# A tuned transformer-layer kernel: own staging tiles for the weights, recurrence steps apart from their norm and gate, another order of the heads' columns

## The chip, the cores and the metric

The kernel runs on one core of a Trainium2 chip. The metric is the device time of one execution in microseconds (us), as the median of several runs. Five engines work side by side and meet only at semaphores: TensorE (PE), VectorE (DVE), ScalarE (ACT), GpSimd (POOL) and SyncE (SP), which issues nearly all DMAs here.

## The reference, cut to what matters

One layer (D = 1024) over 2048 latent rows after a 256-row context. The change touches the first of its three parts, the mixers:

```python
h = modulate(rmsnorm(x, norm_mix), sh1, sc1)
p = h @ w_in                                   # 3584 columns
# A: 4 heads of a gated recurrence, one scan per direction, 128x128 state per head
logf_f, k_f, logf_b, k_b, v = hgrn2_gates(p, ...)
q = silu(p[..., 3*w:4*w]) * HG_DIM ** -0.5
o = rmsnorm(o_f + flip_t(o_b)); o_hg = o * silu(p[..., 4*w:5*w])
# B: 4 heads of a gating unit over chunks of 128 rows
o_mlp = chunk_sgu(p[..., 5*w:6*w], p[..., 6*w:], ...)   # gelu(u) * (W_s LN(gelu(v)) + b)
x = x + g1 * (concat(o_hg, o_mlp) @ w_out)
h2 = modulate(rmsnorm(x, norm_ffn), sh2, sc2)
x = x + g2 * conv_ffn(h2, w_up, conv_w, conv_b, w_down)
```

`g1`, `g2`, `sh1` and so on come from `silu(c) @ w_ada + b_ada`.

## The kernel before, in words

Rows are taken in two halves of 1024 (`hh` 0 and 1). A matmul in full precision is made of three products of split numbers (`mm3`, L128): high part by high part, high by low, low by high. One **pass** of `run_banks` (L503) is one block of 128 columns of `w_in` by 512 rows: 8 slices of k by three products, 24 matmuls of 128x512, into one of three PSUM tiles `pj`. Two passes make a column block of a half. For a head h of group A the blocks are g (the output gate, into `sgt`), t (the values, into `vt`), q (into `qs`) and the two forget gates, four passes in turn, called b here (into `F` and `K`); of group B they are v and u. Before the change the string for a half says `f` for g, t, q in this order (L1071, L1092).

**Weights.** `split_w` (L210) turns 128 columns of `w_in` from a raw tile of 512 KB into `whi` (ScalarE cast, L125) and `wlo` (VectorE difference, L126). There are two such pairs, so a block is split when the pair before the last is free. All raw tiles (`raw_tile`, L200) come from one ring of three, which `w_in` shares with the background work. The load (L207) is traced with the split, unless context columns are near.

**Side work.** Between slices of k, `slot()` (L177) gives two pumps a turn. Each pump holds generators; a generator does a step, then yields a wait in us of PE work (`T.t`, a planned clock of PE alone), after which its next step is due. `hg_q` runs the recurrence of a head (`hg`, L741): score products for seven levels of blocks, each with DVE and ACT updates of Q and K, then transposes, chunk states, a chain over the chunks on DVE (L733, L739), and the outputs. In the first half the outputs of the forward scan, the states of the backward scan, Q and the gate go to DRAM; in the second half `deferred(h)` (L849), a generator of its own behind `hg`, finishes head h of the first half. `o_norm` (L704) squares on ACT, asks POOL for 1/sqrt (L118, L120) and scales on DVE (L713); `o_gate` (L717), 6.5 us later by the pump, transposes and gates. `later(fn, wait)` runs a piece once it is due: the transposes of the values (L576 to L582, due after 2.2), the LayerNorm of group B (`ln`, due after 4.6) and its mixing product (`mix`, 7.0 after that). `bg_q` holds the background: x, then eight blocks of `w_ada`, the taps, `w_down` times g2 (L956, to `wd_d`), `w_out` times g1 and its split (L940, L125, L126, to `wo_d` at L942 and L943).

**Forced steps.** `need(q, what)` runs steps of a pump at once, without their waits, until `what` is done: the keys of the head before at the start of each b (`pre_g`), the scores of the diagonal blocks at q, the end of the head two before at g. `open_wo` (L1103) drains both pumps four passes before the end and then loads the rest of `w_out`; three tiles of it (`wo_early`, L847) are loaded within the last head.

**Order.** The program is traced in this order, and a planner then orders the instructions of each engine by its own estimate of when each is ready; an instruction in `pin(...)` stays behind the one traced before it on its engine. Each engine runs its queue in order, SP too: a store that waits for its data holds back every load behind it. After the first half's last pass, xh and xl, the split rows, are loaded anew from DRAM, 16 loads of 512 KB (L1058, L1059).

Of the kernel before, what the change touches and what calls it, by code (L numbers as in the profile page):

```python
# [18 lines left out]
P = 128  # L19
# [58 lines left out]
def tile_trunk(ctx, tc, x, c, cx, c_ctx, w_ada, b_ada, norm_mix, norm_ffn, w_in, hg_norm, sgu_g, sgu_b,  # L78
# [104 lines left out]
    with es1:  # L183
# [16 lines left out]
        def raw_tile():  # L200
            return p1.tile([P, D], F32, tag="raw", name="raw", bufs=3)
# [3 lines left out]
        def load_raw(key):  # L205
            raw = raw_tile().rearrange("p (k c) -> p k c", c=P)
            ld(raw, w_in[:, key[0]:key[0] + P].rearrange("(k p) c -> p k c", p=P))  # L207
            w_raw[key] = raw

        def split_w(key, eng=None):  # L210
            if key not in w_raw:
                load_raw(key)
            raw, at = w_raw.pop(key), w_free.pop(0)
            hi = p1.tile([P, NK, P], F32R, tag=f"whi{at}", name="whi", align_bytes=AL)
            lo = p1.tile([P, NK, P], F32R, tag=f"wlo{at}", name="wlo", align_bytes=AL)
            split(hi, lo, raw, eng or V)
            return hi, lo, at

# [109 lines left out]
        with tc.manual_schedule():  # L328
# [44 lines left out]
            nxt[0, CTX] = split_w((0, CTX), V)  # L373
# [4 lines left out]
            nxt[HW, CTX] = split_w((HW, CTX), V)  # L378
# [125 lines left out]
        def run_banks(banks, peek=None):  # L504
# [3 lines left out]
            for i, (col, n0, n, sink, pre) in enumerate(banks):  # L508
                if pre is not None:
                    pre()  # L510
                up = list(dict.fromkeys(keys[i:] + tail))
                for key in up[:2]:
                    if key not in nxt:
                        nxt[key] = split_w(key)
# [7 lines left out]
                for k in range(k0, NK):  # L522
                    if k and n == 512:
                        slot()
                    w_products(pj[:, :n], (hi, lo), hiT, loT, sl, k, k + 1)
# [129 lines left out]
        def sgu(hh, h):  # L655
# [14 lines left out]
            def sv(n0, n, pj):  # L670
# [3 lines left out]
                def ln():  # L674
# [10 lines left out]
                    nm = pm.tile([P, 4], F32, tag="nm", name="nm", bufs=2)  # L685
                    V.scalar_tensor_tensor(out=nm, in0=mv[:, :, 0], scalar=-1.0, in1=r[:, :4], op0=ALU.mult, op1=ALU.mult)
                    for i in range(4):
                        S.activation(nt[:, i * P:(i + 1) * P], pt[:, i * P:(i + 1) * P], AF.Identity,
                                     bias=nm[:, i:i + 1], scale=r[:, i:i + 1])

                    def mix():
# [8 lines left out]
                        both(n0)  # L700
                    hg_q.later(mix, 7.0)
# [3 lines left out]
        def o_norm(o):  # L705

            ss = ph.tile([P, 4], F32, tag="oss", name="oss", bufs=2)
            for i in range(4):
# [3 lines left out]
            on = ph.tile([P, 512], F32, tag="on", name="on", bufs=2)  # L712
            V.tensor_mul(on.rearrange("p (c q) -> p c q", q=P), o.rearrange("p (c q) -> p c q", q=P),  # L713
                         view(r, 0, [[1, 4], [0, P]]))
            return on

        def o_gate(hh, h, g0, on, sg):  # L717

            pt = bank("mi")
            for i in range(4):  # L720
                T.transpose(pt[:, i * P:(i + 1) * P], on[:, i * P:(i + 1) * P], ident)
            ot = pm.tile([P, 512], F32, tag="ot", name="ot", bufs=2)
            V.scalar_tensor_tensor(out=ot, in0=pt, scalar=hgn[:, h:h + 1], in1=sg[:, g0:g0 + 512],
                                   op0=ALU.mult, op1=ALU.mult)
            st(oT_d[hh][:, h, g0:g0 + 512], ot)
# [16 lines left out]
        def hg(hh, h, F, K, qs, vt, sgt):  # L742
# [6 lines left out]
            sc = ph.tile([P, NCH, P], F32, tag="S", name="sc")  # L749
# [17 lines left out]
            tot = F  # L767
            for l, B in enumerate(LV):
                if B < SB:
# [28 lines left out]
            yield 2.5  # L798
            fs = ph.tile([P, NCH + 1, P], F32, tag="fs", name="fs")
# [20 lines left out]
            on = []  # L820
            for g in range(0, NCH, 4):
# [9 lines left out]
                if hh == 1:  # L831
                    on.append(o_norm(po))
# [935 lines left out]
```

## Time and profile before

| | us |
|---|---|
| median of 3 runs | 2435.43 (2433.93 to 2435.67) |
| the profiled execution | 2435.89 |
| its span, first to last instruction | 2434.1 |
| projections and mixers (w_in) | about 32 to 952 |
| product with w_out | from about 952 |

The page's shares are averages over three parts with different limits; the change touches the first. PE counts as busy for the modelled length of its matmuls, which overlap, so a PE at 97% has little idle time but says nothing of how dense the rest is. What is lost is read from the waits of PE and from the granted clock, which is 1.00 at 2.4 GHz and 0.50 at 1.2 GHz.

### The profile page before, as it was taken

To read this page: it belongs to the slowest core of one execution; us is meant where nothing else is said; L and a number is where in the kernel's file an instruction comes from. 1 tells how busy PE (TensorE), PEld (TensorE's weight loads), DVE (VectorE), ACT (ScalarE), POOL (GpSimd) and SP (SyncE) were. 2 spreads that over 40 slices of the span, in tenths; PEclk is the share of its full clock that TensorE was granted. 3 is DMA by queue.
4 is the path that set the end of the run, shared out by engine and by line. 5 is a ranking of instruction groups with operands and counts; after the bars stand their busy time and mean duration, and the time that the engine had idled before them with its cause. 6 is when DMAs were issued, how large, how long until landed. Compare 5 with 4: busy or idle time off the path is not lost.

```text
span 2434.1 us, 38863 instructions
## 1 busy us (share of the span) xinstructions
PE 2362.0 (97%) x14951; PEld 1938.0 (80%) x14951; DVE 1703.7 (70%) x2323; ACT 1027.8 (42%) x1776; POOL 791.2 (33%) x739
## 2 busy tenths in 40 slices
PE   6999999999999898999999999999999999999998
PEld 4887887878887777888788888878888878888887
DVE  4656675465577573566898787679999983676876
ACT  4665544444454552454433333333333333332253
POOL 0010000000000121002687878778787860000011
PEclk9999999999999999999999999999999999999999
DMA  8454453563436536678622222552222248843744
GB/s 303 131 191 157 133 166 126 186 216 132 140 130 201 179 109 243 195 217 281 222 93 91 83 89 84 200 212 87 95 84 90 89 162 320 294 135 130 251 153 172
DMA packets 306295, 400.08 MB, mean 164 GB/s; under 512 B 33705, under 2 KB 216753, under 8 KB 302397
## 3 DMA queue, kind: packets, MB, share of 16 engines
q1 hardware_dynamic: 302820, 396.84, 48.8%
q8 instruction: 118, 1.93, 0.3%
q10 hardware_dynamic: 3289, 0.76, 0.1%
q14 instruction: 68, 0.56, 0.1%
HBM read 288.40 MB, written 109.13 MB: 163 GB/s over the span
## 4 chain that ended last, share of the span: by engine, by line
PE 40%; DVE 7%; POOL 2%; issue 2%; DMA 1%; ACT 1%; SPq 0%; POOLq 0%; ACTq 0%; DVEq 0%
PE up L70 23%; PE dn L70 17%; DVE dn L1348 3%; DVE edges L1353 1%; POOL Al L126 1%; DMA raw<-in_w_up_dram 1%; DVE gp L1424 1%; ACT dn L1345 1%; DMA yfar<-yd 0%; POOL raw L1174 0%; DVE keep L1434 0%; DVE keep L1418 0%; ACT cv L1367 0%; POOL fl L1170 0%; ACT Ah L125 0%
## 5 line engine op out<-in xcount | busy, mean ns | idle before, releaser
L1348 DVE SCALAR_TENSOR_TENSOR dn<-gp,taps,dn 128x1024 f32<-128x1024 f32 x352 | 448.1, 1279 | 21.0 <-ACT dn L1345 17.8
L70 PE MATMUL up<-yfar,Ah 128*128 128x512 f32 x1232 | 394.3, 390 | 2.8 <-DMA yfar<-yd 2.8
L70 PE MATMUL dn<-thl,mhl 128*128 128x512 f32 x1680 | 381.0, 389 | 0.0
L70 PE MATMUL pj<-xh,whi 128*128 128x512 f32 x896 | 368.1, 411 | 8.3 <-ACT whi L125 8.2
L126 POOL TENSOR_TENSOR Al<-raw,Ah 128x512 fp32r<-128x512 f32 x264 | 343.7, 1310 | 89.5 <-ACT Ah L125 84.1
L70 PEld LDWEIGHTS dn<-thl,mhl 128*128 128x128 f32 x1680 | 315.3, 188 | 65.5 <-issue 0.2
L70 PE MATMUL pj<-xl,whi 128*128 128x512 f32 x896 | 353.8, 395 | 0.0
L70 PE MATMUL pj<-xh,wlo 128*128 128x512 f32 x896 | 353.6, 395 | 0.2 <-DVE wlo L126 0.2
L70 PE MATMUL up<-xah,Al 128*128 128x512 f32 x704 | 275.9, 392 | 3.7 <-POOL Al L126 3.7
L125 ACT CAST Ah<-raw 128x512 fp32r<-128x512 f32 x264 | 160.4, 618 | 277.4 <-PE up L70 212.7
L70 PE MATMUL up<-xah,Ah 128*128 128x512 f32 x704 | 275.2, 391 | 2.0 <-ACT Ah L125 2.0
L70 PEld LDWEIGHTS up<-yfar,Ah 128*128 128x128 f32 x1232 | 231.4, 188 | 51.3 <-DMA yfar<-yd 3.2
L70 PEld LDWEIGHTS pj<-xh,whi 128*128 128x128 f32 x896 | 170.0, 190 | 45.3 <-ACT whi L125 9.1
L70 PE MATMUL up<-xal,Ah 128*128 128x512 f32 x528 | 205.7, 390 | 0.0
L70 PE MATMUL up<-yfar,Al 128*128 128x512 f32 x528 | 205.2, 389 | 0.0
L70 PEld LDWEIGHTS pj<-xh,wlo 128*128 128x128 f32 x896 | 169.8, 190 | 37.6 <-DVE wlo L126 0.9
L70 PEld LDWEIGHTS pj<-xl,whi 128*128 128x128 f32 x896 | 170.6, 190 | 30.6 <-DVE xl L126 0.2
L70 PE MATMUL dn<-wo,o 128*128 128x512 f32 x768 | 184.7, 397 | 3.7 <-DMA wo<-wo_d 2.8
L70 PEld LDWEIGHTS dn<-wo,o 128*128 128x128 f32 x768 | 143.0, 189 | 34.0 <-DMA wo<-wo_d 3.7
L126 DVE TENSOR_TENSOR wlo<-raw,whi 128x1024 fp32r<-128x1024 f32 x68 | 83.1, 1222 | 121.9 <-ACT whi L125 120.6
L70 PEld LDWEIGHTS up<-xah,Al 128*128 128x128 f32 x704 | 132.6, 188 | 35.5 <-POOL Al L126 8.2
L70 PEld LDWEIGHTS up<-xah,Ah 128*128 128x128 f32 x704 | 132.6, 188 | 30.4 <-ACT Ah L125 3.1
(322 smaller groups left out, 3664.6 us busy)
## 6 DMA issues: line engine op xcount, KB each, us to landing
raw<-in_w_up_dram SPq DMA_DIRECT2D x88, 512.0 KB
mr<-m SPq DMA_DIRECT2D x85, 512.0 KB
raw<-in_w_in_dram SPq DMA_DIRECT2D x68, 512.0 KB
sT<-wd SPq DMA_DIRECT2D x88, 256.0 KB
raw<-in_w_ada_dram SPq DMA_DIRECT2D x32, 512.0 KB
yfar<-yd SPq DMA_DIRECT2D x14, 1024.0 KB
m<-cv SPq DMA_DIRECT2D x22, 544.0 KB
raw<-in_w_down_dram SPq DMA_DIRECT2D x22, 512.0 KB
```

The costliest lines, as they stand in the source:

```text
L70: return self.engine.matmul(out, lhsT, rhs, **kw)
L125: keep(S.copy(hi, raw))
L126: (eng or G).tensor_sub(lo, raw, hi.bitcast(F32))
L1345: S.activation(cr, gt[:, 0:RH, 0:GW], AF.Identity, bias=cvb[:, f:f + 1], scale=taps[:, f:f + 1])
L1348: V.scalar_tensor_tensor(out=cr, in0=gt[:, t // 3:t // 3 + RH, t % 3:t % 3 + GW], scalar=taps[:, t * NF + f:t * NF + f + 1], in1=cr, op0=A ...
L1353: V.scalar_tensor_tensor(out=e[:, 0, :], in0=gt[:, 1, t % 3:t % 3 + GW], scalar=taps[:, t * NF + f:t * NF + f + 1], in1=e[:, 0, :], op0=AL ...
L1424: V.tensor_add(g_rows(hh, f + c, n2), quad(p, kind), quad(add, kind))
```

## The change

- **Raw tiles.** `w_in` uses raw tile 0 alone once the background starts, the background tiles 1 and 2. The raw tile of the block after next is loaded in slice 6 of a pass, if no other raw weight is held.
- **Low part late.** `split_w` casts at the start of a pass; the difference on DVE is traced at slice 3, pinned (`late`), for a block that isn't the pass's own.
- **Norm and gate apart.** `o_out` takes the place of `o_norm` and `o_gate`: squares and 1/sqrt with the step, scaling 3.2 later, transposes and gate 2.6 after that, the store 2.0 after that. In group B, the rows of the LayerNorm that need POOL's result (`rows`) run 3.4 after `ln`. They are pinned.
- **Stores.** Most stores of this part go through `put`: traced pinned some us after their data.
- **First half's finishing in line.** `deferred` becomes the end of `hg(1, h)`, its gate in the `fs` tile; "end" is said behind it, "gated" when its gates are written.
- **Background.** Loads run two ahead and are pinned; each step is cut into smaller ones; g1 is loaded twice in place of 16 times (256 KB each); `w_out` goes by its column half first. `wo_load` now needs all of `w_out`'s preparation (`need(bg_q, "wo")`).
- **need** and `open_wo` also run every piece that `later` holds.
- **Order of columns.** First half: u3 is moved behind b3. Second half: q, t, b and g of a head in that order (for heads 1 to 3 t, q, b, g), and u0 ahead of b3.

The work computed is the same. The diff, cut to its core:

```diff
-        def raw_tile():
-            return p1.tile([P, D], F32, tag="raw", name="raw", bufs=3)
+        raws, turn = {"w": [0, 1, 2], "b": [1, 2]}, {"w": 0, "b": 0}
+
+        def raw_tile(use="b"):
+            turn[use] += 1
+            return p1.tile([P, D], F32, tag=f"raw{raws[use][(turn[use] - 1) % len(raws[use])]}", name="raw")
...
-            raw = raw_tile().rearrange("p (k c) -> p k c", c=P)
+            raw = raw_tile("w").rearrange("p (k c) -> p k c", c=P)
...
-        def split_w(key, eng=None):
+        w_late = []
...
+        def split_w(key, late=False):
...
-            raw, at = w_raw.pop(key), w_free.pop(0)
+            raw, at = w_raw[key], w_free.pop(0)
...
-            split(hi, lo, raw, eng or V)
+            S.copy(hi, raw)
+
+            def low():
+                i = V.tensor_sub(lo, raw, hi.bitcast(F32))
+                if late:
+                    pin(i)
+                del w_raw[key]
+            w_late.append(low)
+            if not late:
...
+        def split_low():
+            while w_late:
+                w_late.pop(0)()
+
+        def put(dst, src, wait=2.5):
+            hg_q.later(lambda: pin(st(dst, src)), wait)
...
                 up = list(dict.fromkeys(keys[i:] + tail))
+                split_low()
                 for key in up[:2]:
                     if key not in nxt:
-                        nxt[key] = split_w(key)
+                        nxt[key] = split_w(key, n == 512 and key != up[0])
...
+                        if k == 3:
+                            split_low()
+                        if k == 6 and len(up) > 2 and up[2] not in nxt and not w_raw:
+                            load_raw(up[2])
...
             while what not in done:
+                if hg_q.soon:
+                    hg_q.flush()
+                    continue
...
-                    st(oT_d[hh][:, 4 + h, n0:n0 + 512], zt)
+                    put(oT_d[hh][:, 4 + h, n0:n0 + 512], zt, 4.0)
...
-                    nm = pm.tile([P, 4], F32, tag="nm", name="nm", bufs=2)
-                    V.scalar_tensor_tensor(out=nm, in0=mv[:, :, 0], scalar=-1.0, in1=r[:, :4], op0=ALU.mult, op1=ALU.mult)
...
-                        S.activation(nt[:, i * P:(i + 1) * P], pt[:, i * P:(i + 1) * P], AF.Identity,
...
+                    def rows():
+                        nm = pm.tile([P, 4], F32, tag="nm", name="nm", bufs=2)
+                        pin(V.scalar_tensor_tensor(out=nm, in0=mv[:, :, 0], scalar=-1.0, in1=r[:, :4], op0=ALU.mult,
+                                                   op1=ALU.mult))
+                        for i in range(4):
+                            pin(S.activation(nt[:, i * P:(i + 1) * P], pt[:, i * P:(i + 1) * P], AF.Identity,
...
+                    hg_q.later(rows, 3.4)
                     hg_q.later(mix, 7.0)
                 hg_q.later(ln, 4.6)
...
-        def o_norm(o):
+        def o_out(hh, h, g0, o, sg, what):
...
-            on = ph.tile([P, 512], F32, tag="on", name="on", bufs=2)
-            V.tensor_mul(on.rearrange("p (c q) -> p c q", q=P), o.rearrange("p (c q) -> p c q", q=P),
...
-            return on
...
+            def scaled():
+                on = ph.tile([P, 512], F32, tag="on", name="on", bufs=2)
+                pin(V.tensor_mul(on.rearrange("p (c q) -> p c q", q=P), o.rearrange("p (c q) -> p c q", q=P),
+                                 view(r, 0, [[1, 4], [0, P]])))
+
+                def gated():
+                    pt = bank("mi")
...
+                    put(oT_d[hh][:, h, g0:g0 + 512], ot, 2.0)
+                    if g0:
+                        done.add(what)
+                hg_q.later(gated, 2.6)
+            hg_q.later(scaled, 3.2)
...
+            sc = None
             for l, B in enumerate(LV):
+                if B == SB:
+                    sc = ph.tile([P, NCH, P], F32, tag="S", name="sc")
...
+            if hh and h and (0, h - 1, "gated") not in done:
+                hg_q.flush()
...
-                st(dh_d[h], bs_[:, :NCH, :].rearrange("p c t -> p (c t)"))
-                st(qb_d[h], Q[:, 0, :])
-                st(sg_d[h], sgt)
+                put(dh_d[h], bs_[:, :NCH, :].rearrange("p c t -> p (c t)"), 1.4)
+                put(qb_d[h], Q[:, 0, :], 1.4)
+                put(sg_d[h], its["sgt"], 1.4)
...
-                    on.append(o_norm(po))
+                    o_out(hh, h, g * P, po, lambda: its["sgt"], (hh, h, "gated"))
...
+                    put(op_d[h][:, g * P:g * P + 512], ot, 2.0)
                 yield 1.0
-            if hh == 1:
-                yield 6.5
-                for g in range(2):
...
+            if hh == 0:
+                return
+            Qb = ph.tile([P, 2, TH], F32, tag="Q", name="Qb", align_bytes=AL)[:, 0, :]
             op = ph.tile([P, TH], F32, tag="S", name="op")
-            bs_ = ph.tile([P, NCH + 1, P], F32, tag="bst", name="bs2")
-            ld(bs_[:, :NCH, :], dh_d[h].rearrange("p (c t) -> p c t", t=P))
-            ld(Qb, qb_d[h])
-            ld(op, op_d[h])
-            ld(sgt, sg_d[h])
...
+            sg = ph.tile([P, NCH + 1, P], F32, tag="fs", name="sg0")[:, :NCH, :].rearrange("p c t -> p (c t)")
...
+            for i, (j, cl) in enumerate(todo):
+                if j == 0:
+                    g = pm.tile([P, 512], F32, tag="acc", name="g2")
+                    pin(ld(g, g_d[1:2, cl].broadcast_to([P, 512])))
+                    yield 4.0
+                raw = raw_.pop(0)
+                pin(V.tensor_mul(raw, raw, view(g, 0, [[0, 2], [1, 512]])))
+                yield 4.0
+                pin(st(wd_d[j][:, :, cl], raw))
+                yield 4.0
+                load(i + 2)
+                yield 2.0
...
+            todo = [(k, slice(n * 512, n * 512 + 512)) for n in range(2) for k in range(NK)]
...
-                    raw = raw_tile()
-                    ld(raw[:, :512], w_out[k * P:(k + 1) * P, cl])
-                    ld(raw[:, 512:], g_d[0:1, cl].broadcast_to([P, 512]))
-                    raws.append(raw)
+                    raw_.append(raw_tile())
+                    pin(ld(raw_[-1][:, :512], w_out[k * P:(k + 1) * P, cl]))
...
+            load(1)
...
+                if k == 0:
+                    g = pm.tile([P, 512], F32, tag="acc", name="g1")
+                    pin(ld(g, g_d[0:1, cl].broadcast_to([P, 512])))
+                    yield 4.0
+                raw = raw_.pop(0)
+                w, hi = raw[:, :512], raw[:, 512:]
                 pin(V.tensor_mul(w, w, g))
-                split(hi.bitcast(F32R), g.bitcast(F32R), w, V)
-                st(wo_d[:, k, 0, cl], hi)
-                st(wo_d[:, k, 1, cl], g)
-                yield 7.0
-
...
+                pin(S.copy(hi.bitcast(F32R), w))
+                yield 1.6
+                pin(V.tensor_sub(w.bitcast(F32R), w, hi))
+                yield 2.2
+                pin(st(wo_d[:, k, 0, cl], hi))
+                pin(st(wo_d[:, k, 1, cl], w))
+                yield 3.0
+                load(i + 2)
...
+            def pre_s():
+                if before[0] >= 0:
+                    need(hg_q, (*before, "gated" if before[0] else "end"))
...
+                    raws["w"] = [0]
+                    bg_q.add(ada_blocks())
                     bg_q.add(conv_taps())
                     bg_q.add(w_down_ops())
-                    bg_q.add(w_out_ops())
+                    bg_q.add(marked(w_out_ops(), "wo"))
...
-                hg_q.add(marked(hg(hh, h, t["F"], t["K"], t["qs"], t["vt"], t["sgt"]), (hh, h, "end")))
-                if hh == 1:
-                    hg_q.add(deferred(h))
...
-        for item in "f1 v2 b1 f2 u2 b2 f3 v3 u3 b3".split():
...
-        run_banks(seq, 4 * HW)
+        rest, post = sequence(0, "b0 g1 t1 q1 v2 b1 g2 t2 q2 u2 b2 g3 t3 q3 v3 b3 u3", ctx_last)
...
+        run_banks(seq, 3 * HW)
...
-        for item in "f0 b0 f1 b1 f2 v0 b2 f3 b3 u0 v1 u1 v2 u2 v3 u3".split():
...
+        seq, post = sequence(1, "q0 t0 b0 g0 t1 q1 b1 g1 t2 q2 v0 b2 g2 t3 q3 u0 b3 g3 v1 u1 v2 u2 v3 u3", post)
...
-            hg_q.drain()
+            while hg_q.tasks:
+                hg_q.flush()
+                hg_q.step()
+            hg_q.flush()
             bg_q.drain()
+            hg_q.flush()
```

## Rows read from the trace of the kernel before

**Rows 1.** The page, part 1: busy us, share of the span and instructions of each engine.

```profile
PE 2362.0 (97%) x14951; PEld 1938.0 (80%) x14951; DVE 1703.7 (70%) x2323; ACT 1027.8 (42%) x1776; POOL 791.2 (33%) x739
```

**Rows 2.** The view of windows, all engines: busy us (xcount), clock, DMA share, GB/s.

```profile
1300.00:1400.00 100.00, 100.00 (x443) 82.84 (x442) 77.08 (x85) 36.45 (x58) 82.58 (x70) 1.00 0.26 85
503.00:511.00 8.00, 6.18 (x19) 4.30 (x18) 5.25 (x6) 3.71 (x4) 0.00 (x0) 0.79 0.62 212
757.00:767.00 10.00, 7.09 (x31) 5.58 (x30) 7.29 (x10) 2.98 (x6) 1.21 (x2) 0.83 0.61 201
822.00:836.00 14.00, 7.38 (x29) 5.94 (x28) 8.27 (x11) 4.19 (x5) 0.00 (x0) 0.76 0.93 276
951.00:965.00 14.00, 10.27 (x40) 7.75 (x40) 1.98 (x2) 1.21 (x3) 1.29 (x1) 0.88 1.04 382
```

**Rows 3.** The view of waits, PE, 480 to 965 us: us, times, longest.

```profile
PE pj L70 <- ACT whi L125: 8.2, 2, 6.6
PE mi L74 <- DVE on L713: 3.7, 4, 1.3
PE mi L74 <- ACT vv L576: 2.9, 1, 2.9
PE dn L70 <- DMA wo<-wo_d: 2.8, 2, 2.3
PE mi L70 <- ACT nt L688: 2.2, 2, 1.5
PE sc L70 <- DVE tot L500: 1.1, 1, 1.1
```

**Rows 4.** The view of waits, the SP queue, 250 to 960 us.

```profile
SPq L942 <- ACT wo_hi L125: 44.6, 13, 15.5
```

**Rows 5.** The view of waits, DVE, 250 to 960 us.

```profile
DVE wlo L126 <- ACT whi L125: 91.3, 22, 15.4
DVE on L713 <- POOL rs L120: 40.4, 16, 7.6
...
DVE nm L686 <- POOL rs L120: 16.1, 12, 2.6
```

**Rows 6.** The timeline, SP, 808 to 828 us: start, us, engine, line.

```profile
822.53 0.39 SPq L207 DMA_DIRECT2D raw<-in_w_in_dram  x1
```

**Rows 7.** The timeline, ACT, 757 to 763 us, then 815 to 834 us.

```profile
761.18 0.62 ACT L125 CAST wo_hi<-raw 128x512 fp32r<-128x512 f32 x1 [2.58 <-DVE raw L940]
761.71 0.58 ACT L576 COPY vv<-pj 128x512 f32<-128x512 f32 x1
...
829.03 1.04 ACT L125 CAST whi<-raw 128x1024 fp32r<-128x1024 f32 x1 [4.35 <-DMA raw<-in_w_in_dram]
```

**Rows 8.** The timeline, DVE, 526 to 552 us, then PE, 533 to 552 us.

```profile
534.63 1.23 DVE L126 TENSOR_TENSOR wlo<-raw,whi 128x1024 fp32r<-128x1024 f32 x1 [2.92 <-ACT whi L125]
...
542.64 1.22 DVE L493 TENSOR_TENSOR Q<-Q,tot 128x1024 f32<-128x1024 f32 x1
...
533.67 0.76 PE L70 MATMUL sc<-Q,K 128*32 128x32 f32 x64
...
548.07 0.40 PE L70 MATMUL pj<-xh,whi 128*128 128x512 f32 x1
```

**Rows 9.** The view of tile `wo_d` on SP: first and last start.

```profile
L943 SPq DMA_DIRECT2D wo_d<-raw x16: 319/320/520, 732.3 to 871.7; - x16
L847 SPq DMA_DIRECT2D wo<-wo_d x8: 319/386/648, 879.5 to 945.3; - x8
```

**Rows 10.** The view of tile `xh` on SP, and the timeline, PE, 503 to 508 us.

```profile
L1058 SPq DMA_DIRECT2D xh<-xh_d x8: 360/365/662, 475.9 to 490.9; - x8
...
505.65 0.50 PE L70 MATMUL pj<-xh,whi 128*128 128x512 f32 x1 [1.62 <-ACT whi L125]
```

**Rows 11.** The view of windows, 480 to 500 us.

```profile
480.00:485.00 5.00, 5.00 (x23) 4.13 (x22) 0.00 (x0) 1.60 (x2) 0.00 (x0) 1.00 1.05 403
...
495.00:500.00 5.00, 5.00 (x84) 3.96 (x83) 1.82 (x2) 0.97 (x2) 0.00 (x0) 1.00 1.05 401
```

More of the change, by code (lines that the diff above doesn't have):

```diff
@@ L798, in hg @@
             yield 2.5
+            if hh and h and (0, h - 1, "gated") not in done:
+                hg_q.flush()
+            vt = its["vt"]
             fs = ph.tile([P, NCH + 1, P], F32, tag="fs", name="fs")
@@ L919, in ada_block @@
-            yield 0.0
+                yield 2.2
+                load(n + 2)
+                if k < 6:
+                    yield 1.4
+                    continue
+                yield 0.6
+                accs.pop()
+                pa = bank("mi")
+                hf_ = e % 2
+                if e in (0, 1, 6, 7):
+                    T.matmul(pa[:1, :], ones[:, :1], acc, start=True, stop=True)
+                    gr = pm.tile([P, 512], F32, tag="ot", name="gr", bufs=2)
+                    S.copy(gr[:1, :], pa[:1, :])
+                    put(g_d[e // 6:e // 6 + 1, hf_ * 512:hf_ * 512 + 512], gr[:1, :], 2.0)
+                else:
+                    for j in range(4):
+                        T.matmul(pa[:, 2 * j:2 * j + 2], acc[:, j * P:(j + 1) * P], ones[:, :2], start=True, stop=True)
+                    if e in (2, 3):
+                        V.tensor_copy(s2[:, hf_ * 4:hf_ * 4 + 4], pa[:, 0:8:2])
+                    else:
+                        V.scalar_tensor_tensor(out=a2[:, hf_ * 4:hf_ * 4 + 4], in0=pa[:, 0:8:2], scalar=1.0,
+                                               in1=nffn[:, hf_ * 4:hf_ * 4 + 4], op0=ALU.add, op1=ALU.mult)
@@ new lines, in ada_blocks, with w_down_ops, load @@
+                yield 1.4
+                open_sum(e + 1)
+                yield 3.0
+        def w_down_ops():
+            todo = [(j, slice(n * 512, n * 512 + 512)) for n in range(2) for j in range(NF // 2)]
+            raw_, g = [], None
+            def load(i):
+                if i < len(todo):
+                    j, cl = todo[i]
+                    raw_.append(raw_tile().rearrange("p (a c) -> p a c", a=2))
+                    pin(ld(raw_[-1], w_down[2 * j * P:2 * (j + 1) * P, cl].rearrange("(a p) c -> p a c", p=P)))
+            load(0)
+            load(1)
+            for i, (j, cl) in enumerate(todo):
[10 more added lines that the diff above has]
+                yield 2.0
@@ L921, in w_out_ops @@
         def w_out_ops():
-            todo = [(k, slice(n * 512, n * 512 + 512)) for k in range(NK) for n in range(2)]
-            raws = []
+            todo = [(k, slice(n * 512, n * 512 + 512)) for n in range(2) for k in range(NK)]
+            raw_, g = [], None
             def load(i):
@@ L985, in pre_g @@
                 if prev[0] >= 0:
-                    need(hg_q, (prev[0], prev[1], "keys"))
+                    need(hg_q, (*prev, "keys"))
                 else:
                     need(bg_q, "x1")
-                    for e in range(8):
-                        bg_q.add(ada_block(e))
+                    raws["w"] = [0]
+                    bg_q.add(ada_blocks())
                     bg_q.add(conv_taps())
                     bg_q.add(w_down_ops())
-                    bg_q.add(w_out_ops())
+                    bg_q.add(marked(w_out_ops(), "wo"))
                 t["F"] = pk.tile([P, 2, TH], F32, tag="F", name="F", align_bytes=AL)
```

206 lines of the change are left out of this document (81 added, 125 removed).

## The prediction

> **What bounds the kernel now.** First the page's part 1: PE is busy for 97% of the span and DVE, next, for 70% (PE's weight loads, 80%, lie beside its matmuls) [rows 1], so time is lost only where PE waits or runs at the lower clock. An undisturbed stretch gives PE's pace, 443 matmuls in 100 us, 0.226 us each [rows 2]; a pass of 24 takes 5.4 us. The change alters nothing behind the mixers (952 us on), and ahead of 480 us lie the context part, the x rows and the first heads, whose order hardly changes; so I read the waits of PE from 480 to 965 us. The ones shown add up to 20.9 us [rows 3], and each long one is followed by a stretch at the lower clock. A clock mean of 0.76 over 14 us is 0.24 x 14 = 3.4 us lost, and so 1.7 us each around 505, 760 and 958 us [rows 2]. Waits and clock together, about 29 us, are nearly all that the change can win.
>
> Next, who is late. The SP queue stood 44.6 us on stores of the background's cast, one of them 15.5 us [rows 4], with later loads behind it. DVE stood 91.3 us at `wlo` for its cast, and 40.4 and 16.1 us at `on` and `nm` for POOL's 1/sqrt [rows 5]. These queues aren't the bound, but what is queued behind such a wait may be what PE needs.
>
> **The change part by part.** The sum is made against the profiled execution, 2435.9 us, which lies 0.5 us above the median.
>
> *Raw tiles, loads early, stores late.* The longest wait of PE is for the first weight of u0. Its load was issued at 822.53, behind stores that waited [rows 6], and the cast began at 829.03, having waited for that load [rows 7]. It is late since the background holds two of the three tiles of the ring and the load is traced only with the split. In the changed kernel `w_in` has a tile of its own, and while b's four passes hold both weight pairs the load goes out more than two passes (12 us) earlier; SP no longer stands at `wo_hi` stores, which are traced 3.8 us behind their cast. I take the whole 6.6 us and the 3.4 of the clock: **-10.0**.
>
> *The background in smaller steps.* The second wait, for `vv` (2.9 us), came from ACT's own queue: the cast `wo_hi` stood 2.58 us for `raw` L940, which lacked its load, and `vv` was next [rows 7]. Loads two ahead, and a product and cast traced together behind a landed load, take this away: 2.9 + 1.7 = **-4.6**. Fourteen fewer loads of g1 go away, which no engine of the bound waits for: nothing.
>
> *Late low part.* It removes DVE's stand at `wlo` [rows 5], which PE doesn't feel; I price the gain at nothing. It is a risk too: pinned at slice 3, the difference for b's second block stands behind every level update forced at b's start. In the trace `wlo` ran at 534.63, ahead of them; the last update of Q ran at 542.64, so a pinned `wlo` would end at 542.64 + 1.22 + 1.23 = 545.1, and PE needs it at 548.07 [rows 8]: 3.0 us of margin. The Trainium skill, TensorE: Matmul & The Clock Gate, its table of the engine, calls the queues of ScalarE, VectorE and GpSimd strictly first in, first out; the stand at `vv` agrees, and by the rule the pinned difference can't pass a late update. For this, and for pieces that hold a PSUM tile 3 us longer until their scaling, I take **+2.0** (between 0 and 7 x 1.2, a `wlo` at each b behind a recurrence).
>
> *Norm and gate apart.* DVE's 56.5 us behind POOL go away; PE felt of it the 2.2 us at `nt`, the 3.7 at `on` and perhaps the 1.1 at `tot` [rows 3]. The waits for `on` belong to the drain of `open_wo`, which still runs scaling and gate at once: they stay. Of `nt` and `tot`, 3.3, I take **-2.0**.
>
> *First half in line; the end.* By the yields a head of the second half, with its finishing, took 87 us of PE work before it ended and takes 70 now, while ten passes and its own products give some 75. So before, each head began late and more steps were forced (b2, b3, `open_wo`); now the queue keeps up, and the last head stands about a pass further on at `open_wo`. The last loads of `wo`, issued at up to 945.3 [rows 9], then start some 5 us earlier and the 2.8 us of PE at `wo` go, with 1.7 of the clock: **-4.5** (0 if they stay late).
>
> *The new wait for "wo".* Behind it stand the rest of the last head and all of `open_wo`. The preparation's last store was issued at 871.7 [rows 9]. By the yields the last head will come to its first `wo` load about a pass ahead of `open_wo`, five passes (27 us) and its own products ahead of 952, near 900. The preparation's new yields sum to 35 us less but are cut into 82 more steps, each up to 0.7 us late, so it ends at about the same place, 30 us ahead: nothing; otherwise the blocks left would run unspaced.
>
> *Order of the columns.* The second half's xh and xl are 16 loads of 512 KB, 8.4 MB, and their columns come free as the last passes use them. Now b is last, so columns 0 to 511 come free two passes before columns 512 on: the loads run from 475.9 to about 500 [rows 10], at 400 GB/s with every DMA engine busy [rows 11], so 20.7 us of DMA. PE nearly notices: the load of a weight behind them makes it wait 1.62 us at 505.65 [rows 10]. With u3 last, the first columns come free one pass, 5.4 us, later, and the second are needed as early as before. Everything behind shifts by up to 5.4 us; in return, the next head's first two score products, 0.76 us each [rows 8], now come ahead of that point. Taken: 5.4 - 1.5 = **+3.9** (from -3.3, if the weight's load is put ahead and today's wait and its clock go, to +7.1, with another 1.7 of clock). The Trainium skill, Perfetto Trace Analysis, Roofline, gives 16 engines about 435 GB/s in all; the trace shows 403. By that figure the reload is an estimated 1.4 us shorter and this term 2.5.
>
> *need flushes.* When keys are forced, what `later` holds now runs too. At v3-b3 and v0-b2 that is a LayerNorm and its mixing product, begun one pass earlier. If the planner lets PE go on with b, it costs little: **+2.0**. Its upper bound is the second rival.
>
> Sum: -10.0 - 4.6 + 2.0 - 2.0 - 4.5 + 3.9 + 2.0 = -13.2. 2435.9 - 13.2 = 2422.7, less 0.5 for the median: **2422 us**.
>
> **The rivals.** *A. Only the weight goes.* The waits at `vv`, `nt` and `wo` depend on where the planner puts ACT and SP work, and may return at other places, as queues that are pinned can't be evened out. Then -10.0, with 5.4 for the reload and the 2.0 of the flush: -2.6, 2433. For it: DVE and ACT still do the same work. Against: each of these waits has a named cause that the diff removes.
>
> *B. Slower: the flush inside need.* Between a LayerNorm and its mixing product the code leaves 7.0 us of PE work, and even so PE waited up to 1.5 us for `nt` [rows 3]. Run at once ahead of b, with `rows` pinned, PE has nothing in its place: 7.0 + 1.5 + 3.4 of clock (as behind the 6.6 us wait) = 11.9 us, at v3-b3 and v0-b2; at t0-b0 the values' transposes, 2.9 + 1.7. Together 28.4 in place of 2.0: 2422 + 26 = 2448. It decides the sign from 15 us on. Against it: transposes, mixing and b's products aren't pinned on PE, so the planner may let b's products go ahead of them.
>
> *C. Nothing moves.* The planner orders by readiness, and the order on the engines may stay much as it was: 2435.
>
> **How the numbers follow.** The forecast has 0.62, A 0.18, B 0.14, C 0.06. A measurement of this kernel can tell about 0.2%, 4.9 us, from no change. Faster is the forecast, 0.62; same is A and C, 0.24; slower is B, 0.14. The forecast's own range goes from 2407 (all the waits shown and their clock won, little lost) to 2430. Stretched over A and C it ends at 2438; B's upper part and a little below are left out.
>
> **What would show it.** Right: no PE wait for `whi` over 1 us near u0, and its load issued passes ahead; none for `vv`; SP's stand at `wo_hi` gone; DVE's at `on` and `nm` gone; the loads of `wo` before 940; a wait of PE of 3 to 7 us at the start of the second half, for xh, xl or `whi`. Wrong: waits of PE at the start of b for `nt`, `vv` or `wlo` (B), or a wait for a weight elsewhere, which the tile of its own was to prevent.

## The result and the profile after

The changed kernel takes **2437.55 us** (median of 12 runs, 2433.91 to 2442.86), the kernel before 2433.17 in the same comparison (12 runs, 2429.28 to 2435.67): a ratio of **1.0018** [1.0011, 1.0026]. That is within the 0.2% that the prediction called no change, on the slow side of it, and 15.5 us above the 2422 forecast. The profiled execution of the changed kernel (2435.09 us, span 2433.2) lies 2.5 us below its median and the one of before (2435.89, span 2434.1) 2.7 us above the median of these 12. So the two traces are level, and the 4.4 us between the medians can't be looked for in their difference.

The page's part 1 of the changed kernel (busy us, share of the span and instructions of each engine) answers to [rows 1]:

```profile
PE 2361.6 (97%) x14951; PEld 1935.2 (80%) x14951; DVE 1706.3 (70%) x2323; ACT 1033.7 (42%) x1780; POOL 791.8 (33%) x739
```

PE has the same matmuls and the same busy time. What matters is which waits it has. The view of waits of the changed kernel, PE, 480 to 965 us (us, times, longest), answers to [rows 3]:

```profile
PE mi L74 <- DVE on L748: 7.7, 7, 1.4
PE pj L70 <- DMA xl<-xl_d: 4.7, 6, 1.1
PE mi L70 <- ACT nt L720: 4.5, 4, 1.9
PE pj L70 <- ACT whi L221: 1.6, 1, 1.6
PE mi L74 <- ACT kt L834: 1.5, 2, 0.9
PE sc L70 <- ACT K L595: 1.4, 1, 1.4
...
PE dn L70 <- DVE nt L728: 0.8, 1, 0.8
...
PE pj L70 <- DMA xh<-xh_d: 0.3, 1, 0.3
```

Read it against [rows 3] line by line. The 6.6 us of u0's weight and the 2.9 at `vv` are gone, as forecast. The 2.8 at `wo` are gone too, but not because the loads come earlier: they come later, and the product with `w_out` begins at 957.1 us instead of 953.3. In their place stand 5.0 us for `xl` and `xh`, 4.0 more at `on` and 2.3 more at `nt`. All the waits of that view add up to 24.5 us, and to 26.0 in the kernel before: for the most part they changed places. The stands of the other engines went, in part: the view of waits of the changed kernel, DVE, 250 to 960 us, for [rows 5]:

```profile
DVE wlo L224 <- ACT whi L221: 41.7, 13, 6.5
DVE on L748 <- POOL rs L120: 36.9, 13, 7.6
...
DVE nm L717 <- POOL rs L120: 14.0, 11, 1.5
```

`wlo` fell from 91.3 to 41.7 us, but `on` only from 40.4 to 36.9 and `nm` from 16.1 to 14.0: the gap that the code leaves between the norm's parts seems shorter than what it must cover (an experiment below widens it). SP's stand at the cast of `w_out` fell from 44.6 [rows 4] to 17.6 us.

Now the start of the second half, where the new waits are. The view of windows of the changed kernel (busy us and count of PE, PEld, DVE, ACT, POOL, then clock, DMA share, GB/s):

```profile
500.00:505.00 5.00, 3.59 (x12) 2.09 (x12) 0.32 (x1) 0.60 (x1) 0.00 (x0) 1.00 1.04 386
505.00:510.00 5.00, 3.59 (x12) 2.09 (x12) 0.38 (x1) 0.00 (x0) 0.00 (x0) 1.00 1.05 404
510.00:515.00 5.00, 3.15 (x11) 1.91 (x11) 0.00 (x0) 0.02 (x1) 0.00 (x0) 1.00 1.08 377
515.00:520.00 5.00, 2.08 (x4) 1.17 (x4) 3.09 (x4) 3.80 (x4) 0.00 (x0) 0.60 0.21 81
520.00:525.00 5.00, 4.95 (x73) 4.09 (x74) 4.27 (x6) 0.76 (x2) 0.00 (x0) 0.50 0.55 179
```

At the undisturbed pace of 0.226 us [rows 2] PE does 22 products with 512 columns in 5 us; here it does 12, 12 and 11, with every DMA engine busy at 377 to 404 GB/s. The transfer sets the pace. Just behind it the granted clock falls to half (1.2 GHz) and stays there until about 526 us. The timeline of PE (start, us, engine, line, operation, idle before and releaser) shows the pattern, a wait at every sixth product, one pair of loads later each time, and then the weight:

```profile
502.59 0.50 PE L70 MATMUL pj<-xl,whi 128*128 128x512 f32 x1 [0.78 <-DMA xl<-xl_d]
...
505.52 0.49 PE L70 MATMUL pj<-xl,whi 128*128 128x512 f32 x1 [0.73 <-DMA xl<-xl_d]
...
508.12 0.50 PE L70 MATMUL pj<-xl,whi 128*128 128x512 f32 x1 [0.78 <-DMA xl<-xl_d]
...
516.56 0.80 PE L70 MATMUL pj<-xh,whi 128*128 128x512 f32 x1 [1.62 <-ACT whi L221]
```

In the kernel before, the loads of `xh` began at 475.9 [rows 10] and the DMA engines ran at some 400 GB/s from 480 to 500 [rows 11] beneath a PE that was busy all the time. In the changed kernel, by the view of tile `xh` on SP and SP's timeline, they begin 10.4 us later, and in the middle SP waits 4.2 us to issue a store:

```profile
L1122 SPq DMA_DIRECT2D xh<-xh_d x8: 419/487/851, 486.3 to 501.3; - x8
```

```profile
487.29 0.46 SPq L1123 DMA_DIRECT2D xl<-xl_d  x1
491.94 0.33 SPq L238 DMA_DIRECT2D oT<-nt  x1
...
492.94 0.62 SPq L1122 DMA_DIRECT2D xh<-xh_d  x1
```

The granted clock is down for about as long in all: windows of 5 us from 180 to 970 us show some 20 us at half clock in either kernel. The places moved, from u0 and `vv` to the reload (some 10 of the 20 us lie between 515 and 530). This isn't all lost time, since the clock is down for a part of PE's waits too.

### The profile page after: what moved, and what is told of

The parts are those of the page before. It is cut to its first block, busy times and chain, and to the rows that moved or that the text cites. A ratio compares the mean times of both kernels' runs of the same rounds, so it can differ in the third digit from the quotient of the medians.

```text
span 2433.2 us, 38825 instructions
## 1 busy us (share of the span) xinstructions
PE 2361.6 (97%) x14951; PEld 1935.2 (80%) x14951; DVE 1706.3 (70%) x2323; ACT 1033.7 (42%) x1780; POOL 791.8 (33%) x739
## 4 chain that ended last, share of the span: by engine, by line
PE 40%; DVE 7%; POOL 2%; issue 2%; DMA 2%; ACT 1%; SPq 0%; POOLq 0%; ACTq 0%; DVEq 0%
PE up L70 22%; PE dn L70 17%; DVE dn L1407 3%; DVE edges L1412 1%; POOL Al L126 1%; DVE gp L1483 1%; DMA raw<-in_w_up_dram 1%; ACT dn L1404 1%; DMA yfar<-yd 0%; POOL raw L1233 0%; POOL cv L1494 0%; DVE keep L1493 0%; DVE keep L1477 0%; DMA xn<-cv 0%; DMA m<-cv 0%
```

## The experiments

All variants were timed in five rounds against the kernel before. Its medians were 2432.77 beside the first four, 2432.47 beside the next four and 2434.33 beside the last three. The ratios on record differ by up to 0.0009 (2 us) from the quotients of these medians, so differences between variants are good to some 2 us.

| kernel | us | ratio to before |
|---|---|---|
| the change | 2437.55 | 1.0018 [1.0011, 1.0026] |
| u3_back | 2426.48 | 0.9974 [0.9965, 0.9982] |
| put_free | 2437.62 | 1.0024 [1.0015, 1.0033] |
| before_u3_last | 2444.08 | 1.0045 [1.0032, 1.0058] |
| no_flush | 2433.50 | 1.0004 [0.9995, 1.0013] |
| raw_only | 2421.99 | 0.9950 [0.9935, 0.9964] |
| end_loose | 2420.17 | 0.9941 [0.9928, 0.9955] |
| wider | 2422.52 | 0.9950 [0.9936, 0.9964] |
| old_columns | 2428.45 | 0.9980 [0.9971, 0.9989] |
| no_raw | 2427.86 | 0.9972 [0.9963, 0.9981] |
| joined | 2415.22 | 0.9922 [0.9908, 0.9936] |
| joined_early | 2411.06 | 0.9905 [0.9891, 0.9919] |

**The order u3, b3.** First the changed kernel with b last again in the first half (u3_back), and the kernel before with u3 last (before_u3_last).

```diff
-        rest, post = sequence(0, "b0 g1 t1 q1 v2 b1 g2 t2 q2 u2 b2 g3 t3 q3 v3 b3 u3", ctx_last)
+        rest, post = sequence(0, "b0 g1 t1 q1 v2 b1 g2 t2 q2 u2 b2 g3 t3 q3 v3 u3 b3", ctx_last)
```

> The changed kernel with the first half's last blocks as before (v3 u3 b3 in place of v3 b3 u3), nothing else. Theory R (the reload of the split rows between the halves, begun one pass later by the new order and held up by SP, eats the gain): PE's waits for xl and xh between 495 and 530 us (5.0 us) and the 10 us at the lower clock behind them go; the time falls by about 10 us against the changed kernel, to about 2427, 0.997 of the kernel before. Theory N (norm and gate in line and their waits for on and nt, 12 us from 530 us on, eat it): the time stays within 3 us of the changed kernel, about 1.001.

```diff
-        for item in "f1 v2 b1 f2 u2 b2 f3 v3 u3 b3".split():
+        for item in "f1 v2 b1 f2 u2 b2 f3 v3 b3 u3".split():
```

> The kernel before with u3 behind b3, nothing else. Theory R: the reload's late start alone costs it what it costs the changed kernel; waits for xh or xl appear near 500 us and the time rises by 6 to 10 us, 1.003 to 1.004 of the kernel before. If the cost lay in the pinned stores alone (P), there are no such waits and the time stays within 3 us, up to 1.001.

Two words swapped in a string cost 11.1 us in the changed kernel (2437.55 - 2426.48) and 11.3 in the kernel before (2444.08 - 2432.77). Both ways agree, so this price doesn't hang on the rest of the change. Its place is seen in before_u3_last, view of waits, PE, 495 to 530 us, where [rows 10] had the 1.62 for the weight alone:

```profile
PE pj L70 <- DMA xl<-xl_d: 5.4, 5, 1.7
PE pj L70 <- ACT whi L125: 1.6, 1, 1.6
```

and in u3_back, where the waits of PE, 480 to 965 us, and two windows stand beside the changed kernel's:

```profile
PE mi L74 <- DVE on L748: 7.7, 7, 1.4
PE mi L70 <- ACT nt L720: 4.5, 4, 1.9
PE pj L70 <- ACT whi L221: 1.6, 1, 1.6
PE pj L70 <- issue: 1.4, 1, 1.4
...
PE pj L70 <- DMA xl<-xl_d: 0.7, 1, 0.7
PE sc L70 <- ACT K L595: 0.7, 1, 0.7
```

```profile
515.00:520.00 5.00, 5.00 (x43) 3.88 (x45) 4.29 (x7) 2.85 (x4) 0.00 (x0) 1.00 0.46 154
520.00:525.00 5.00, 5.00 (x86) 4.24 (x76) 4.28 (x7) 1.36 (x3) 0.00 (x0) 1.00 0.77 263
```

At this place the changed kernel waits 4.7 + 0.3 + 1.6 + 1.4 = 8.0 us and u3_back 0.7 + 1.6 + 1.4 + 0.7 = 4.4; between 515 and 525 us the clock of the one lacks 0.4 x 5 + 0.5 x 5 = 4.5 us (one less the granted clock, times the window's length) and that of the other nothing. That makes 8.1 us of the 9.4 between the two spans (2433.2 and 2423.8), as an upper bound, since from 515 to 520 PE was busy for 2.08 us only, so that much of the lower clock fell into waits. The waits at `on` and `nt` are the same to a tenth.

The make-up isn't fixed. In before_u3_last the waits at this place rise by 5.4 us (1.6 to 7.0), and the clock from 505 to 525 lacks no more than in the kernel before (1.7 us); the rest of its 11.3 isn't placed. In put_free, below, which has the changed kernel's order and time, the waits there are 9.3 us and the clock lacks 1.75 (520 to 530). What the runs show is the price and its place, not a split into waits and clock.

**The store's pin.** A rival read the gap in SP's loads, and the late loads at the end, as the work of the stores that `put` pins to their place.

```diff
-            hg_q.later(lambda: pin(st(dst, src)), wait)
+            hg_q.later(lambda: st(dst, src), wait)
```

> The changed kernel, whose late stores are traced at the same places but not pinned, so that the planner may put loads ahead of them on SP. Theory P (stores pinned on SP hold back the loads behind them: the split rows at 487 to 492 us, the last head's finishing at 920 to 928 us): both stands go, 4 us at the reload and 5 at the end; about 2430, 0.998 to 0.999 of the kernel before. If R alone holds, the time falls by no more than 3 us, since the one pass is lost in any case: 1.000 to 1.002.

2437.62: nothing. The trace shows why: without their pins the stores keep their places. The one among the reload's loads is issued at 493.03 behind a wait of 3.9 us, and two at the end stand for 7.12 us at 921.47, ahead of the loads of the deferred head. So this run shows that the pins themselves cost nothing, and doesn't test the order of the queue; for the end, the run of the end below does.

**The flush inside need** (the forecast's rival B, 28 us). Pieces of `later` are run inside `need` for "gated" alone, or when no other step is left.

```diff
-                if hg_q.soon:
+                if hg_q.soon and (what[-1] == "gated" or not q.tasks):
```

> The changed kernel, whose need doesn't run the pieces held by later (but where what is asked for is itself such a piece). The rival of the prediction (the flush inside need holds PE at v3-b3, v0-b2 and t0-b0): the time falls by 8 us or more, to 0.998 or less. Theories R, N and P: no change over 3 us against the changed kernel, 1.001 to 1.003.

2433.50, 4 us below the change by median and 3.4 by ratio; the intervals overlap a little (1.0013 and 1.0011). A few us, no more, where rival B asked for 8 or more here: it is refuted.

**The raw tiles alone.** The kernel before with a raw tile of its own for `w_in`, the load at slice 6 and the low part at slice 3, and nothing else. (The three weren't told apart.)

```diff
-            return p1.tile([P, D], F32, tag="raw", name="raw", bufs=3)
+            return p1.tile([P, D], F32, tag=f"raw{raws[use][(turn[use] - 1) % len(raws[use])]}", name="raw")
...
-                        nxt[key] = split_w(key)
+                        nxt[key] = split_w(key, n == 512 and key != up[0])
...
+                        if k == 3:
+                            split_low()
+                        if k == 6 and len(up) > 2 and up[2] not in nxt and not w_raw:
+                            load_raw(up[2])
...
+                    raws["w"] = [0]
```

> The kernel before with the raw tiles apart, the load at slice 6 and the late low part alone; stores, norm, gate, background steps and orders as before. If this part earned what the prediction gave it, PE's 6.6 us wait for u0's weight and the 3.4 us of clock go: about 2423, 0.996 of the kernel before. If the load is held back all the same by the stores of the background that stand on SP ahead of it, the wait shrinks but stays and the ratio is 0.998 to 1.000.

2421.99, 10.5 us below before. The timelines of raw_only, SP, ACT and PE, show the weight of [rows 6, 7]: loaded 17.7 us earlier, cast 10.4 us earlier, and PE's pass on it held for a third of a microsecond:

```profile
804.80 0.38 SPq L210 DMA_DIRECT2D raw<-in_w_in_dram  x1
```

```profile
818.59 1.06 ACT L221 CAST whi<-raw 128x1024 fp32r<-128x1024 f32 x1
```

```profile
824.04 0.50 PE L70 MATMUL pj<-xh,wlo 128*128 128x512 f32 x1 [0.36 <-DVE wlo L224]
```

Its waits of PE, 480 to 965 us, have no `vv` either, though the background's steps are the old ones:

```profile
PE mi L74 <- DVE on L736: 3.7, 4, 1.3
PE mi L70 <- DMA Qb<-qb: 1.6, 1, 1.6
PE pj L70 <- ACT whi L221: 1.6, 1, 1.6
```

**The end.** In `open_wo` the changed kernel runs held pieces and steps by turns. Here all steps come first and then the pieces, on top of u3_back.

```diff
-            while hg_q.tasks:
-                hg_q.flush()
-                hg_q.step()
+            hg_q.drain()
             hg_q.flush()
```

> u3_back, whose open_wo runs all steps of hg_q first and then what later holds, in place of what later holds ahead of each step. Theory E (in the drain the pinned stores of the last head's gates stand on SP ahead of the four loads of its finishing, 927.7 us in the changed kernel against 921.7 in the kernel before): the loads go out 4 to 6 us earlier against the start of u0's passes and the product with w_out begins 3 to 5 us earlier; about 2422, 0.9955. If PE covers this time anyway, within 2 us of u3_back, 0.997.

2420.17 against 2426.48, 6.3 us. The two timelines of SP show what moved; u3_back first:

```profile
909.66 7.12 SPq L238 DMA_DIRECT2D oT<-ot  x2
916.88 0.38 SPq L888 DMA_DIRECT2D bs<-dh  x1
...
918.28 0.43 SPq L888 DMA_DIRECT2D sg<-sg  x1
...
937.54 3.00 SPq L906 DMA_DIRECT2D wo<-wo_d  x5
```

and end_loose:

```profile
910.08 0.32 SPq L888 DMA_DIRECT2D bs<-dh  x1
...
911.40 0.43 SPq L888 DMA_DIRECT2D sg<-sg  x1
...
923.62 6.08 SPq L238 DMA_DIRECT2D oT<-ot  x4
...
930.88 2.41 SPq L906 DMA_DIRECT2D wo<-wo_d  x4
```

In u3_back two stores of the last gates stand for 7.1 us ahead of the four loads that the finishing of the last head begins with. Drained first, these loads go 6.8 us earlier, the loads of `wo` 6.7 and the product with `w_out` starts at 942.2 instead of 945.5. Counted from the pass behind b3 (826.6 and 823.2, by PE's products), it starts 6.7 us earlier, 115.6 us instead of 122.3, which agrees with the 6.3. (The spans of the two profiled executions differ by 2.6 only: one lies 0.9 us below its median, the other 2.8 above.) The changed kernel shows the same 7.11 us of `oT<-ot` at 920.47, its loads at 927.68 to 929.07.

**The gaps of norm and gate.** With norm and gate apart, the yields promise 3.2 us of PE work between the squares and the scaling. The chain it has to cover (squares, POOL's 1/sqrt, scaling) kept DVE idle for 2.8 us a time even so (36.9 us in 13 waits at `on`). Wider gaps, on top of u3_back:

```diff
-                    hg_q.later(rows, 3.4)
-                    hg_q.later(mix, 7.0)
+                    hg_q.later(rows, 4.6)
+                    hg_q.later(mix, 9.0)
...
-                hg_q.later(gated, 2.6)
-            hg_q.later(scaled, 3.2)
+                hg_q.later(gated, 3.6)
+            hg_q.later(scaled, 4.4)
```

> u3_back with longer spaces: scaling after 4.4 (not 3.2), gate 3.6 after that (2.6), rows after 4.6 (3.4), mixing product after 9.0 (7.0). Theory G (the new spaces are shorter than the chain of squares, POOL and scaling takes, so PE waits 3.4 us for on within the heads and some 2 for nt): these waits go, the four of the drain stay; 2422 to 2424, 0.9955 to 0.9965. Rival: the longer spaces hold PSUM tiles and delay the ends of the heads, new waits come: within 2 us of u3_back or slower.

2422.52, 4.0 us below u3_back. PE waits for `on` four times, 5.1 us, instead of seven, 7.7 (the four belong to the drain at the end); the waits at `nt` didn't shrink (5.0 instead of 4.5). So part of the mechanism holds, that for `on`; its 2.6 us are not all of the 4.0.

**The order of the second half**, the old one on u3_back (g, t, q, b of a head, u0 behind b3; the first block of the second half, whose weight is split ahead of the reload, is then g0 and not q0):

```diff
-        run_banks(seq, 3 * HW)
+        run_banks(seq, 4 * HW)
...
-        seq, post = sequence(1, "q0 t0 b0 g0 t1 q1 b1 g1 t2 q2 v0 b2 g2 t3 q3 u0 b3 g3 v1 u1 v2 u2 v3 u3", post)
+        seq, post = sequence(1, "g0 t0 q0 b0 g1 t1 q1 b1 g2 t2 q2 v0 b2 g3 t3 q3 b3 u0 v1 u1 v2 u2 v3 u3", post)
```

> u3_back with the second half's columns as before (g t q b; u0 behind b3). By the prediction the order of the second half's blocks is worth nothing by itself: within 3 us of u3_back, 0.9965 to 0.9985. If b3 and u0 in their new order is what took the wait at u0 away, that wait comes back: 2433 or more, 1.000.

2428.45, 2 us above u3_back with intervals that overlap. Next to nothing, and u0's wait doesn't come back with it: with the raw tiles apart it stays away in either order.

**All but the raw tiles**, on end_loose: one ring of three again, the load with the split, the low part at once.

```diff
-            return p1.tile([P, D], F32, tag=f"raw{raws[use][(turn[use] - 1) % len(raws[use])]}", name="raw")
+            return p1.tile([P, D], F32, tag="raw", name="raw", bufs=3)
...
-                        nxt[key] = split_w(key, n == 512 and key != up[0])
+                        nxt[key] = split_w(key)
...
-                        if k == 6 and len(up) > 2 and up[2] not in nxt and not w_raw:
-                            load_raw(up[2])
```

> end_loose without the raw tiles apart: one ring of three tiles, the load with the split and the low part at once, as in the kernel before; all else as in end_loose (2420, 0.9941). Theory W (the tile of the weights' own is what earns, the apart norm and gate, late stores and small background steps earn little): it comes back to 2428 to 2432, 0.998 to 1.000. Rival: the late stores alone keep SP free for the weights' loads, so the ring costs nothing: within 3 us of end_loose, 0.994 to 0.995.

2427.86, 7.7 us above end_loose and 6.5 below the kernel before. So neither reading was right as it stood: the other parts do earn something by themselves, once the order and the end are put right, and the raw tiles are worth 7.7 us on top of them where they were worth 10.5 alone. Some 3 us are the same microseconds, won by either: the waits of PE for `whi` in no_raw, 480 to 970 us, are 2.4 us in two, the longest 1.7, so the 6.6 at u0 stay away without the tile too. Which of the other parts does this, and which earns the 6.5, wasn't tried.

**Everything that helped.** `joined` is u3_back with the edits of end_loose, wider and no_flush. `joined_early` also traces the load of the second half's second weight ahead of the reload of `xh` and `xl`:

```diff
         run_banks(seq, 3 * HW)
+        load_raw((2 * HW, 512))
         for q in range(0, TH, 512):
```

> u3_back, end_loose, wider and no_flush together: u3 ahead of b3, the drain without pieces between its steps, the longer spaces, need without the flush. If the four gains are of different places: 6 us of the drain, 4 of the spaces and 0 to 4 of the flush below u3_back, 2414 to 2418, 0.992 to 0.994. If they share one place (the last head), about as end_loose, 0.994.

> joined, with the load of the second half's second weight traced ahead of the reload of the split rows: if PE's 1.6 us wait for whi near 505 us comes from that load's place behind the reload, it goes with its stretch at the lower clock, 1 to 3 us, 0.991 to 0.993; if the planner keeps the load where it was, no difference to joined.

2415.22 and 2411.06: both beat both kernels, the second by 23 us (0.95%) against the kernel before. By the medians the three edits gave 11.3 us together over u3_back; one by one, 6.3, 4.0 and some 4. The last step gave 4.2, more than the 1 to 3 expected. In joined_early the weight's load was issued at 488.18, among the reload's (497.46 in joined), and the list of PE's waits, 480 to 965 us, no longer has `whi`:

```profile
PE mi L74 <- ACT kt L834: 3.0, 3, 2.6
PE pj L70 <- issue: 2.5, 1, 2.5
PE mi L74 <- DVE on L748: 1.6, 3, 0.7
PE mi L70 <- DVE bs L776: 0.9, 1, 0.9
PE mi L70 <- ACT nt L720: 0.9, 1, 0.9
```

All waits of PE from 480 to 970 us add up to 10.6 us in both kernels (others came in its place); what went is the lower clock, 3.4 us in joined's windows from 500 to 520 and none in joined_early's. The timeline of ACT says what the 1.62 us for `whi` are, in joined:

```profile
509.37 0.60 ACT L1022 ACTIVATE sig<-pj 128x512 f32<-128x512 f32 x1 [6.47 <-PE pj L70]
509.86 1.04 ACT L221 CAST whi<-raw 128x1024 fp32r<-128x1024 f32 x1
```

and in joined_early:

```profile
493.97 1.05 ACT L221 CAST whi<-raw 128x1024 fp32r<-128x1024 f32 x1 [0.83 <-DMA raw<-in_w_in_dram]
```

In joined the cast stands in ACT's queue right behind `sig`, which waits for the pass that PE has just ended. So it does in the kernel before (504.06, 504.56), in the changed one and in u3_back, and so the wait is 1.62 us in each. With the load ahead the cast comes before that.

## Why the prediction failed, step by step

Forecast 2422 us, measured 2437.55. Its sum was -13.2, the measured difference +4.4. The two longest waits that it named went; what failed are the price of the order of columns, the end, which the drain holds back, and the sign of norm and gate apart. One gain was counted twice.

- **Order of the columns, +3.9: measured +11.** This is the step that turned the result, and the price lies beyond its own upper bound of 7.1. The place, the waits for `xh`, `xl` and `whi` (3 to 7 us foretold, 6.6 in the changed kernel) and a lower clock behind them were foretold; the sum "everything behind shifts by up to 5.4 us" was not enough. That the reload comes one pass later was right: counted from the first product of the second half (490.7 us before, 493.0 in u3_back, 494.1 in before_u3_last, 495.5 in the changed kernel, by PE's products), its first load goes out 14.8 and 15.0 us ahead with b3 last, and 10.5 in both kernels with u3 last.

  PE then takes each pair of column blocks as it lands, stopping some 0.8 us at each, so that nearly two passes run at half pace, and the clock falls behind them. Why 4.4 us at the load become 11 at the end stays open in part. In both kernels with u3 last SP waits for stores `oT<-nt` among these loads, once in the changed kernel (4.2 us) and twice in before_u3_last (7.8). In the changed kernel the DMA engines were busy meanwhile (share 0.83 to 1.05 in windows of 1 us, 487 to 492), so little was lost by it there; in before_u3_last the share from 495 to 500 fell to 0.72.

  The rate wasn't at fault: the transfer ran at 377 to 404 GB/s, nearly the 401 to 409 of before. The Trainium skill, Perfetto Trace Analysis, Roofline, has 435 for 16 engines; no window of 5 us in the reload shows it, and by it the term would have come out smaller still. The prediction also read the 1.62 us for `whi` as the load's; the cast stands behind `sig` on ACT, as shown above.
- **Raw tiles, -10.0: -10.5 in raw_only.** Right in place and mechanism; that the sizes agree so well is partly luck. The 10.5 also hold the 2.9 at `vv` and other waits: all waits of PE from 480 to 970 us fall by 10.5 (26.0 to 15.5), which alone would be the whole, and the windows lack 5.1 us of clock instead of 10.2, so something else grew by some 5 us. And the 3.4 of clock that the sum added counts about 1 us twice: in the kernel before the clock is down from 828 us on, and PE stood still until 830.13, a time that is in the 6.6 already.
- **Background in smaller steps, -4.6: not its own.** The wait at `vv` has gone in raw_only too, whose background is the old one. ACT's stand behind a late `raw` was a matter of the shared ring, or of the moment at which u0's weight pushed the rest; the 10.5 hold it. What the smaller steps do alone wasn't tried.
- **Late low part, +2.0: about nothing.** No wait for `wlo` is in the changed kernel's list; in raw_only they are 0.6 us, in two. The margin of 3.0 us held.
- **Norm and gate apart, -2.0: wrong sign.** The waits at `on` rose from 3.7 to 7.7 and at `nt` from 2.2 to 4.5. I took the scaling to be late no more, since it is issued apart; but 3.2 us of PE work don't cover squares, 1/sqrt and scaling, and what was one late step is now several. DVE's stands at `on` and `nm`, which were to go, are still 36.9 and 14.0 us. Wider gaps win 4.0 us.
- **First half in line, the end, -4.5: not there.** The last load of `wo` was issued at 950.9, not ahead of 940 (945.3 before). From the pass behind b3 to the product with `w_out` the trace has 123.2 us in the kernel before and in the changed one, and 122.3 in u3_back: at most 0.9 won of 4.5. The step that failed was that a last head which stands further on brings its loads forward: they stand in the SP queue behind stores that the drain traces ahead of them. 6.3 us come back when the drain is turned round. The prediction had put the drain's way of running held pieces at nothing, though it had said itself that what is queued behind such a wait may be what PE needs.
- **need flushes, +2.0: some 3 to 4, with intervals that overlap.** B's 28 us don't exist. **The wait for "wo", 0:** no stand was seen.
- **Ahead of 480 us,** priced at nothing: PE's waits from 180 to 480 are 6.6 us in the changed kernel and 4.3 before, and the clock from 185 to 195 lacks 1.75 us where it lacks none before. That is one execution of each; some of it may be chance.
- **The rivals.** A said that waits "may return at other places", and that came true at `on` and `nt`; its sum had 5.4 us for the reload, half of what it cost. The time lies inside the range, at its upper edge (2438), which was drawn for A and C; it came there by other ways than theirs.

How the price splits: the runs form a chain, before, no_raw (-6.5), end_loose (-7.7), u3_back (+6.3), the change (+11.1). These add up to +3.2 by construction, so the sum checks nothing (it is 2437.55 less 2434.33, the third median of before; the first comparison had +4.4). Along this chain the change holds about 14 us of gain and 17 of loss. Another chain would split it in another way, as the 10.5 and 7.7 of the raw tiles show.

## What to carry to other kernels

When an operand is reloaded whole between two phases, look at which work uses it last and how long the transfer has: here 20 us of DMA at full rate lay hidden beneath four passes, and one swap of the last two pieces put it on the path. On a queue that keeps its order, a store that waits for its data makes every load behind it wait as long (7.1 us at the end here), so what begins the next chain is traced ahead of what ends the last. A load on which the bound engine depends is best issued early, into a buffer that no background work can hold; those edits by themselves won 10.5 us, where the whole change lost 4.4.

## What the runs showed that was not expected

With the DMA engines pacing PE by waits of 0.3 to 1.1 us, most of them at every sixth product, the granted clock stayed at 1.00 for the 15 us of it (500 to 515), with PE at half its pace, and fell only around the longer stop at 516.56, to stay at 1.2 GHz through 525 us. In u3_back, with 29 products between 500 and 510 us instead of 24, the same stop of 1.62 us for the weight, at 510.32, came without a fall (1.00 in each window up to 525). At 187 us PE stops for some 3 us in the kernel before without a fall (1.00 in the windows from 180 to 200), and for 2.8 in the changed one with 0.83 and 0.82 in the windows from 185 to 195. So the prediction's habit of adding 1.7 or 3.4 us of clock to each long wait fits the wait at u0, but isn't a property of the wait alone.
